# Shared PSUM bank for two transposes, head 0's weight sums on VectorE, and a later mLSTM turn

## Chip, cores and metric

The kernel runs on one core of a Trainium2 chip. The metric is the device time of one execution in microseconds (us), as the median of several runs.

## What is computed

One layer with two branches on the same RMS-normalised input (512 positions and 16 learned meta tokens, width 1024), merged by gates and projected:

```python
h = rms_norm(x, g_pre)
z = h @ w_in
(fq, fk, fv, ff, fz, mqk, mv, mi, mf, mo, mz, ga, gb) = jnp.split(z, SPLIT_POINTS, axis=-1)
...
ya = (oa * jax.nn.silu(fz)) @ w_a
...
hb = rms_norm(hb, g_head.reshape(MLSTM_HEADS, MLSTM_V_DIM)).reshape(B, L, MLSTM_WIDTH)
yb = (hb * jax.nn.silu(mz)) @ w_b
merged = jax.nn.sigmoid(ga) * ya + jax.nn.sigmoid(gb) * yb
return x + rms_norm(merged @ w_o, g_post)
```

`oa` is FoX attention: 8 heads of 128, softmax of scaled scores with a learned decay, in query chunks of 128. `hb` is the mLSTM: 4 heads with a matrix memory, in chunks of 128.

## The kernel before

Everything is float32, and each product is made of three matmuls of high and low parts (`mm3`, lines 149 to 152: high by high, high by low, low by high). Weights come by DMA on SP's queue into a ring of four raw buffers (`wload`, lines 122 to 129); ScalarE writes the high part, and VectorE subtracts it from the raw one for the low part (lines 142 and 144, and `split`, lines 250 and 252).

Many projections are Strassen units for 256 columns of the weights. `st_narrow` (from line 255) makes sums of blocks of the weights: two additions by the engine `adder` (lines 260 and 261) and two on VectorE (266 and 267); its splits are named `a`, `b`, `c` and `d`. `st_products` then runs seven products of 12 matmuls each, X, Y, Z, W, Y', X', Z', into two PSUM banks: X and Y use the second bank, Z and W the first. ScalarE takes snapshots of partial results: line 314 of the second bank after Y (Y' writes it again), 318 of the first after W, 322 of the second after X'. VectorE combines them at the end (325, 326, 328).

PSUM has eight banks, all of one pool and one tag (`psum1`); a new tile takes the bank that comes free first and waits until its last reader is done. A scheduler turns the program into one order for each engine, and an engine runs its instructions in that order. So both the order of the code and the bank that a tile happens to get set who waits for whom.

The first half of the program is the mLSTM, head by head. `mz_part` (lines 764 to 779) makes the gate `z` with two Strassen units for each head; `value_part` (781 to 813) makes the head's result (its matmuls are lines 790 to 792, from `w`, `wh` and `wl` of lines 728 to 731); `turn_part` (815 to 828) transposes the result on PE (821), multiplies it by the gate (824) and splits it (825, 826); and `wb_part` multiplies it by `w_b`. In head 0 ScalarE's line 742 evicts four banks `po`.

The second half is FoX attention, two heads at a time (`p` from 0 to 3, `m` 0 and 1). `fq_part`, `fk_part` and `fv_part` make queries, keys and values. `prob_part` reads the score banks `pl` on VectorE (line 972), takes the exponential on ScalarE (977) and writes probabilities `pn` on GpSimd and VectorE (980, 982). `ptr_part` (986 to 1006) transposes them on PE, chunk by chunk (996, and 997 for the meta tokens into `pmt`), and ScalarE and VectorE evict each chunk as high and low part (1001, 1002; 1003 and 1004 for `pmt`). `fout_part` multiplies them by the values (1016 to 1019, evicted by 1020). Between these stand Strassen units: `fz_part`, with a sigmoid on ScalarE (925) and a product on VectorE (926), and the gates `ga` and `gb` (`gate_part`, sigmoid in line 932). The seam between the halves is the code from `bt = turn_part(*pend)` on: the last head's transposes, the first `fq` unit, the first `fk`, `ga_part(0)`, `wb_part` of the last head and `gb_part(0)`.

```python
for c in range(NCH):
    o = OFFP[c]
    pt = psum1(f"pt{h}{c}")
    for j in range(c + 1):
        T.transpose(pt[:, j * P:(j + 1) * P], pn[:, o + P + j * P:o + P + (j + 1) * P], ident)
    T.transpose(pmt[:, c * P:(c + 1) * P], pn[:, o:o + P], ident)
```

Of the kernel before, what the change touches and what calls it, by code (L numbers as in the profile page):

```python
# [12 lines left out]
ALU = mybir.AluOpType  # L13

P = 128
# [11 lines left out]
MV = 512  # L27
# [5 lines left out]
C_MO, C_MZ, C_GA, C_GB = 8208, 10256, 12304, 13328  # L33
# [20 lines left out]
def tile_hybrid_block(ctx: ExitStack, tc: tile.TileContext, x, meta, norm_pre, norm_post, w_in, b_fox_f,  # L54
                      conv_w, conv_b, b_i, b_f, g_head, w_a, w_b, w_o, out):
    nc = tc.nc
    V, S, G, T = nc.vector, nc.scalar, nc.gpsimd, nc.tensor
# [8 lines left out]
    def f(ap):  # L66
        return ap.bitcast(F32)

    def psum1(name):
        return pa.tile([P, 512], F32, tag="pa", name=name)  # L70

    def banks(name, n):

        return [psum1(f"{name}_{i}") for i in range(n)]
# [6 lines left out]
    ident = cp.tile([P, 224], F32, name="ident")[:, 0:P]  # L81
# [16 lines left out]
    def sb(shape, dt, tag, name, pool=None, **kw):  # L98

        n = 1  # L100
        for d in shape[1:]:
            n *= d
        size = BYTES.get(tag, 4096)
        t = (pool or wk).tile([shape[0], size // (2 if dt == BF16 else 4)], dt, tag=tag, name=name, **kw)[:, 0:n]
        if len(shape) == 3:
            t = t.rearrange("p (a b) -> p a b", a=shape[1])
        elif len(shape) == 4:
            t = t.rearrange("p (a b c) -> p a b c", a=shape[1], b=shape[2])
        return t
# [23 lines left out]
    def wchunk(*args):  # L133

        return wsplit(wload(*args))
# [24 lines left out]
    def proj_t_all(ps, w, m, t0=0):  # L160

        n = (L - t0) // 2
        for u in range(2):
            s0 = t0 + u * n
            for k in range(KC):
                mm3(ps[u][:, 0:n], w[0](k, m * P, m * P + P), w[1](k, m * P, m * P + P),
                    hh[:, k, s0:s0 + n], hl[:, k, s0:s0 + n], k == 0, k == KC - 1)
# [121 lines left out]
    def st_products(o, units):  # L289


        begun = set()

        def prod(d, w, t):
            (wh_, wl_), (th, tl) = o[w], TB[t]
            for m, (wz, yx, _, ts) in enumerate(units):
                bank = wz if d in "WZ" else yx
                dst = bank[:, 0:256] if d in "WY" else bank[:, 256:512]
                first = (m, d in "WZ") not in begun
                begun.add((m, d in "WZ"))  # L300
                for k in range(4):
                    st, sp = first and k == 0, k == 3
                    if ts is None:
                        mm3(dst, wh_[:, k, :], wl_[:, k, :], th[:, k, :], tl[:, k, :], st, sp, skip_group_check=True)
                    else:
                        mm3(dst, th[:, k, ts], tl[:, k, ts], wh_[:, k, :], wl_[:, k, :], st, sp, skip_group_check=True)

        def halves(bank):
            return bank.rearrange("p (s n) -> p s n", s=2)

        prod("X", "a11", "b11")
        prod("Y", "s3", "t3")
        for wz, yx, snap, _ in units:
            S.activation(snap[:, 0:2], halves(yx), AF.Copy)
        prod("Z", "s1", "t1")
        prod("W", "a12", "b21")
        for wz, yx, snap, _ in units:
            S.activation(snap[:, 3], wz[:, 256:512], AF.Copy)
        prod("Y", "a22", "t4")
        prod("X", "s2", "t2")  # L320
        for wz, yx, snap, _ in units:
            S.activation(snap[:, 2], yx[:, 256:512], AF.Copy)
        prod("Z", "s4", "b22")
        for wz, yx, snap, _ in units:
            V.tensor_tensor(yx[:, 256:512], snap[:, 0], yx[:, 256:512], ALU.subtract)
            V.tensor_tensor(halves(yx), halves(yx), snap[:, 2:4], ALU.subtract)
        for wz, yx, snap, _ in units:
            V.tensor_tensor(halves(wz), halves(wz), snap[:, 1:3], ALU.add)
# [432 lines left out]
    def st_unit(c0, name, room, adder=V, into=None):  # L761

        ps = banks(f"p{name}", 2)
        st_products(st_narrow(c0, f"w{name}", adder, into), [(ps[0], ps[1], room.rearrange("p a (b n) -> p (a b) n", b=2), None)])
        return ps

    def mz_part(h, u):
        g = sb([P, 2, SEQ], F32, ("qk1h", "qk1l")[u], f"gz{h}{u}")
        into = None
        if u:  # L770
            t = sb([P, 2, 4, P], F32R, "sg", f"wz{h}{u}a", gp)
            into = t[:, 0], t[:, 1]
        ps = st_unit(C_MZ + h * MV + u * 256, f"z{h}{u}", g, G, into)
        for m in range(2):
            S.activation(g[:, m, :], ps[m], AF.Sigmoid)
        for m in range(2):
            mi = 80 + h * 4 + u * 2 + m
            V.scalar_tensor_tensor(g[:, m, :], ps[m], gc[:, mi:mi + 1], g[:, m, :], ALU.mult, ALU.mult)
        return g
# [34 lines left out]
    def turn_part(h, hts, gz):  # L814
        bh = sb([P, 4, SEQ], F32R, "big_h", f"bh{h}")
        bl = sb([P, 4, SEQ], F32R, "big_l", f"bl{h}")
        for c in range(NCH):
            pt = psum1(f"pht{h}{c}")
            pv = pt.rearrange("p (e t) -> p e t", e=4)
            for e_ in range(4):  # L820
                T.transpose(pv[:, e_, :], hts[c][:, e_ * P:(e_ + 1) * P], ident)
            y = sb([P, 4, P], F32, "y", f"yt{h}{c}", bufs=2)
            for u in range(2):
                V.tensor_tensor(y[:, 2 * u:2 * u + 2, :], pv[:, 2 * u:2 * u + 2, :], gz[u][:, :, c * P:(c + 1) * P], ALU.mult)
            S.activation(bh[:, :, c * P:(c + 1) * P], y, AF.Copy)
            V.tensor_tensor(bl[:, :, c * P:(c + 1) * P], y, f(bh[:, :, c * P:(c + 1) * P]), ALU.subtract)
        return bh, bl
# [19 lines left out]
    pend = None  # L847
    tokens = st_tokens()
    next(tokens)
    for h in range(MH):  # L850
        if pend is not None:
            bt = turn_part(*pend)
# [8 lines left out]
        if h == 0:  # L861
            v = v0
            ps = banks("pv01", 2)
# [19 lines left out]
        pend = (h, hts, gz)  # L883


    def fq_part(p):
        ps = st_unit(C_FQ + p * 256, f"fq{p}", sb([P, 2, SEQ], F32, "w", f"fqs{p}"))
        s = -(FD ** -0.5)
        qh = sb([P, 2, SEQ], F32R, "qk0h", f"fqh{p}")
        ql = sb([P, 2, SEQ], F32R, "qk0l", f"fql{p}")  # L890
        for m in range(2):
            S.activation(qh[:, m, :], ps[m], AF.Copy, scale=s)
            V.scalar_tensor_tensor(ql[:, m, :], ps[m], s, f(qh[:, m, :]), ALU.mult, ALU.subtract)
        return qh, ql

    def fk_part(p):
        w = wchunk(win, 0, KC, C_FK + p * 256, 256, f"wfk{p}")
        kh = sb([P, 2, L], F32R, "qk1h", f"fkh{p}")
        kl = sb([P, 2, L], F32R, "qk1l", f"fkl{p}")
        for m in range(2):  # L900
            ps = banks(f"pfk{p}{m}", 2)
            proj_t_all(ps, w, m)
            for u in range(2):
                hv = kh[:, m, u * HL:u * HL + HL]
                S.activation(hv, ps[u][:, 0:HL], AF.Copy)
                V.tensor_tensor(kl[:, m, u * HL:u * HL + HL], ps[u][:, 0:HL], f(hv), ALU.subtract)
        return kh, kl
# [77 lines left out]
    def ptr_part(p, m, pn):  # L985
        h = 2 * p + m
        pth = sb([P, NCH, SEQ], F32R, "big_h", f"pth{h}")
        ptl = sb([P, NCH, SEQ], F32R, "big_l", f"ptl{h}")
        ptm = sb([P, SEQ], F32R, "ptm", f"ptm{h}", gp)
        pmt = psum1(f"pmt{h}")  # L990
        pts = []
        for c in range(NCH):
            o = OFFP[c]
            pt = psum1(f"pt{h}{c}")
            for j in range(c + 1):
                T.transpose(pt[:, j * P:(j + 1) * P], pn[:, o + P + j * P:o + P + (j + 1) * P], ident)
            T.transpose(pmt[:, c * P:(c + 1) * P], pn[:, o:o + P], ident)
            pts.append(pt[:, 0:(c + 1) * P].rearrange("p (j t) -> p j t", t=P))
        for c, pv in enumerate(pts):
            dst = pth[:, 0:c + 1, c * P:(c + 1) * P]  # L1000
            S.activation(dst, pv, AF.Copy)
            V.tensor_tensor(ptl[:, 0:c + 1, c * P:(c + 1) * P], pv, f(dst), ALU.subtract)
        S.activation(ptm, pmt, AF.Copy)
        V.tensor_tensor(ptm[96:128, :], pmt[96:128, :], f(ptm[96:128, :]), ALU.subtract)
        return pth, ptl, ptm
# [24 lines left out]
        V.tensor_tensor(gl, yb[:, 2 * p:2 * p + 2, :], f(gh), ALU.subtract)  # L1030
        return gh, gl

    bt = turn_part(*pend)
    d_yb = [dram.tile([P, 2, SEQ], F32, name=f"d_yb{u}") for u in range(4)]
    d_sa = [dram.tile([P, 2, SEQ], F32, name=f"d_sa{u}") for u in range(3)]
    q = fq_part(0)
    k = fk_part(0)
    ga_part(0)
    wb_part(MH - 1, bt)
# [83 lines left out]
    pn = banks("pout", NCH)  # L1123
# [7 lines left out]
    for u in (2, 3):  # L1131
        w = wchunk(wo, 0, KC, u * 256, 256, f"wo{u}")
        for b in range(NCH):
            ps = psum1(f"pout{u}{b}")
# [40 lines left out]
```

## Time and profile before

| what | value |
|---|---|
| median of three runs | 946.1 us (945.33 to 946.22) |
| the profiled execution | 945.64 us, span 943.9 us |
| PE busy | 916.6 us, 97% of the span |
| VectorE (DVE) busy | 667.8 us, 71% |
| ScalarE (ACT) busy | 476.0 us, 50% |
| GpSimd (POOL) busy | 148.9 us, 16% |
| mean granted clock of PE | 0.992 of full speed |

The span runs from the first to the last instruction of the profiled execution; its own time has 1.7 us around it. In the rows further down, a line of a timeline gives the start, the length, the engine, the line of the program, the operation, the tiles (written <- read), the shape and, in brackets, how long the engine stood idle just before and whose result ended that. Several equal instructions in a row are one line with their number (x4). `PEclk` is the granted clock of PE as a share of full speed.

### The profile page before, as it was taken

To read this page: it belongs to the slowest core of one execution; us is meant where nothing else is said; L and a number is where in the kernel's file an instruction comes from. 1 tells how busy PE (TensorE), PEld (TensorE's weight loads), DVE (VectorE), ACT (ScalarE), POOL (GpSimd) and SP (SyncE) were. 2 spreads that over 40 slices of the span, in tenths; PEclk is the share of its full clock that TensorE was granted. 3 is DMA by queue.
4 is the path that set the end of the run, shared out by engine and by line. 5 is a ranking of instruction groups with operands and counts; after the bars stand their busy time and mean duration, and the time that the engine had idled before them with its cause. 6 is when DMAs were issued, how large, how long until landed. Compare 5 with 4: busy or idle time off the path is not lost.

```text
span 943.9 us, 15725 instructions
## 1 busy us (share of the span) xinstructions
PE 916.6 (97%) x6296; PEld 848.3 (90%) x6296; DVE 667.8 (71%) x1112; ACT 476.0 (50%) x818; POOL 148.9 (16%) x190
## 2 busy tenths in 40 slices
PE   8999799999999999999999999989999989999997
PEld 6998699889998899988999989889998989998887
DVE  6988678538887378874688757587885687895634
ACT  5746456435565255662465425455763554773331
POOL 3055100122001211012020002111321121300000
PEclk9999899999999999999999999999999999999999
DMA  7323132412333133233133335124362224348402
GB/s 229 92 71 108 45 112 73 121 42 76 104 113 93 53 90 90 91 101 90 26 109 90 113 111 158 52 75 135 90 193 75 75 67 135 97 169 317 139 23 90
DMA packets 73539, 97.47 MB, mean 103 GB/s; under 512 B 5237, under 2 KB 56533, under 8 KB 73466
## 3 DMA queue, kind: packets, MB, share of 16 engines
q1 hardware_dynamic: 71400, 92.76, 32.1%
q0 software_dynamic: 576, 2.10, 0.6%
q10 hardware_dynamic: 1490, 1.61, 0.5%
q8 instruction: 49, 0.80, 0.3%
q14 instruction: 24, 0.20, 0.1%
HBM read 90.62 MB, written 5.83 MB: 102 GB/s over the span
## 4 chain that ended last, share of the span: by engine, by line
PE 76%; DVE 11%; ACT 6%; issue 2%; POOL 2%; DMA 2%; POOLq 0%; DVEq 0%; ACTq 0%; SPq 0%
PE pyb L152 3%; PE pyb L150 3%; PE pyb L151 3%; PE pz L150 3%; PE pz L151 3%; PE pz L152 3%; PE pqk L150 3%; PE pqk L152 3%; PE pqk L151 3%; PE pv L152 3%; PE pv L150 3%; PE pv L151 3%; PE po L152 2%; PE po L151 2%; PE po L150 2%
## 5 line engine op out<-in xcount | busy, mean ns | idle before, releaser
L980 POOL TENSOR_SCALAR pn<-lt,rsum 128x128 f32<-128x128 f32 x32 | 28.4, 891 | 136.2 <-DVE rsum L978 99.5
L151 PE MATMUL pyb<-bl,wb_h 128*128 128x512 f32 x128 | 49.8, 389 | 0.0
L152 PE MATMUL pyb<-bh,wb_l 128*128 128x512 f32 x128 | 49.8, 389 | 0.0
L150 PE MATMUL pyb<-bh,wb_h 128*128 128x512 f32 x128 | 49.8, 389 | 0.0
L151 PE MATMUL pv<-wv_l,hh 128*128 128x512 f32 (+1 forms) x128 | 46.5, 364 | 1.5 <-DVE wv_l L144 1.5
L152 PE MATMUL pv<-wv_h,hl 128*128 128x512 f32 (+1 forms) x128 | 46.4, 363 | 0.0
L150 PE MATMUL pv<-wv_h,hh 128*128 128x512 f32 (+1 forms) x128 | 46.4, 362 | 0.0
L695 DVE SCALAR_TENSOR_TENSOR y<-z,gc,y 128x512 f32<-128x512 f32 (+1 forms) x48 | 36.2, 759 | 2.2 <-ACT y L688 1.5
L150 PE MATMUL pqk<-hh,wq_h 128*128 128x258 f32 x128 | 36.4, 284 | 0.0
L150 PE MATMUL pfk<-hh,wfk_h 128*128 128x264 f32 x128 | 36.3, 284 | 0.0
L150 PE MATMUL pqk<-hh,wk_h 128*128 128x264 f32 x128 | 36.3, 284 | 0.0
L151 PE MATMUL pfk<-hl,wfk_h 128*128 128x264 f32 x128 | 36.3, 284 | 0.0
L152 PE MATMUL pqk<-hh,wk_l 128*128 128x264 f32 x128 | 36.3, 283 | 0.0
L152 PE MATMUL pfk<-hh,wfk_l 128*128 128x264 f32 x128 | 36.3, 283 | 0.0
L151 PE MATMUL pqk<-hl,wk_h 128*128 128x264 f32 x128 | 36.2, 283 | 0.0
L152 PE MATMUL pqk<-hh,wq_l 128*128 128x258 f32 x128 | 36.0, 282 | 0.0
L151 PE MATMUL pqk<-hl,wq_h 128*128 128x258 f32 x128 | 36.0, 282 | 0.0
L151 PEld LDWEIGHTS pv<-wv_l,hh 128*128 128x128 f32 x128 | 24.1, 189 | 5.6 <-DVE wv_l L144 1.7
L845 DVE TENSOR_TENSOR yb<-pyb,yb 128x512 f32<-128x512 f32 x24 | 16.5, 688 | 17.4 <-PE pyb L152 17.4
L152 PEld LDWEIGHTS pyb<-bh,wb_l 128*128 128x128 f32 x128 | 24.0, 188 | 5.0
L151 PEld LDWEIGHTS pyb<-bl,wb_h 128*128 128x128 f32 x128 | 24.0, 188 | 4.9
L150 PEld LDWEIGHTS pyb<-bh,wb_h 128*128 128x128 f32 x128 | 24.0, 188 | 4.8
(1806 smaller groups left out, 3659.3 us busy)
## 6 DMA issues: line engine op xcount, KB each, us to landing
wv_r<-in_w_in_dram SPq DMA_DIRECT2D x16, 512.0 KB, 4.7
wo_r<-in_w_in_dram SPq DMA_DIRECT2D x16, 512.0 KB, 4.2
wz_r<-in_w_in_dram SPq DMA_DIRECT2D x16, 512.0 KB, 4.0
wb_r<-in_w_b_dram SPq DMA_DIRECT2D x16, 512.0 KB, 3.5
ab<-d_na SPq DMA_DIRECT2D x8, 672.0 KB, 4.0
wq_r<-in_w_in_dram SPq DMA_DIRECT2D x8, 512.0 KB, 3.7
wk_r<-in_w_in_dram SPq DMA_DIRECT2D x8, 512.0 KB, 4.2
wfq_r<-in_w_in_dram SPq DMA_DIRECT2D x8, 512.0 KB, 3.7
```

What stands on the lines that cost most here:

```text
L150: T.matmul(ps, ah, bh, start=start, stop=False, **kw)
L151: T.matmul(ps, ah, bl, start=False, stop=False, **kw)
L152: T.matmul(ps, al, bh, start=False, stop=stop, **kw)
L695: V.scalar_tensor_tensor(y[:, t0:L], z[:, m, t0 + j:L + j], gc[:, j * 16 + mi:j * 16 + mi + 1], y[:, t0:L], ALU.mult, ALU.add)
L845: V.tensor_tensor(dst, ps[i], dst, ALU.add)
L980: G.tensor_scalar(pn[:, o:o + P].rearrange("p (g t) -> p g t", g=4), lt[:, 0:32].unsqueeze(1).to_broadcast([P, 4, 32]), rsum, None, ALU.mult)
```

## The change

It has three parts. In `mz_part` the two units of head 0 make their additions of lines 260 and 261 on VectorE instead of GpSimd. In `ptr_part` the transposes of query chunks 0 and 1 go into one PSUM bank instead of two, with one filler transpose for the empty corner, and are evicted as one block of 2 x 256 instead of one of 128 and one of 256. And the last head's `turn_part` stands behind the first `fq` unit instead of ahead of it.

```diff
--- before.py
+++ after.py
@@ -770,7 +770,7 @@
         if u:
             t = sb([P, 2, 4, P], F32R, "sg", f"wz{h}{u}a", gp)
             into = t[:, 0], t[:, 1]
-        ps = st_unit(C_MZ + h * MV + u * 256, f"z{h}{u}", g, G, into)
+        ps = st_unit(C_MZ + h * MV + u * 256, f"z{h}{u}", g, G if h else V, into)
         for m in range(2):
             S.activation(g[:, m, :], ps[m], AF.Sigmoid)
         for m in range(2):
@@ -991,15 +991,21 @@
         pts = []
         for c in range(NCH):
             o = OFFP[c]
-            pt = psum1(f"pt{h}{c}")
+
+            if c != 1:
+                pt = psum1(f"pt{h}{c}").rearrange("p (j t) -> p j t", t=P)
             for j in range(c + 1):
-                T.transpose(pt[:, j * P:(j + 1) * P], pn[:, o + P + j * P:o + P + (j + 1) * P], ident)
+                T.transpose(pt[:, 1 + 2 * j if c == 1 else j, :], pn[:, o + P + j * P:o + P + (j + 1) * P], ident)
+                if c == 1 and j == 0:
+                    T.transpose(pt[:, 2, :], pn[:, o + P:o + P + P], ident)
             T.transpose(pmt[:, c * P:(c + 1) * P], pn[:, o:o + P], ident)
-            pts.append(pt[:, 0:(c + 1) * P].rearrange("p (j t) -> p j t", t=P))
-        for c, pv in enumerate(pts):
-            dst = pth[:, 0:c + 1, c * P:(c + 1) * P]
+            pts.append(pt)
+        pt2 = pts[1].rearrange("p (j c) t -> p j (c t)", j=2)
+        for pv, dst, low in ((pt2, pth[:, 0:2, 0:2 * P], ptl[:, 0:2, 0:2 * P]),
+                             *((pts[c][:, 0:c + 1], pth[:, 0:c + 1, c * P:(c + 1) * P],
+                                ptl[:, 0:c + 1, c * P:(c + 1) * P]) for c in (2, 3))):
             S.activation(dst, pv, AF.Copy)
-            V.tensor_tensor(ptl[:, 0:c + 1, c * P:(c + 1) * P], pv, f(dst), ALU.subtract)
+            V.tensor_tensor(low, pv, f(dst), ALU.subtract)
         S.activation(ptm, pmt, AF.Copy)
         V.tensor_tensor(ptm[96:128, :], pmt[96:128, :], f(ptm[96:128, :]), ALU.subtract)
         return pth, ptl, ptm
@@ -1030,10 +1036,10 @@
         V.tensor_tensor(gl, yb[:, 2 * p:2 * p + 2, :], f(gh), ALU.subtract)
         return gh, gl
 
-    bt = turn_part(*pend)
     d_yb = [dram.tile([P, 2, SEQ], F32, name=f"d_yb{u}") for u in range(4)]
     d_sa = [dram.tile([P, 2, SEQ], F32, name=f"d_sa{u}") for u in range(3)]
     q = fq_part(0)
+    bt = turn_part(*pend)
     k = fk_part(0)
     ga_part(0)
     wb_part(MH - 1, bt)
```

The lines of `ptr_part` and of what follows it move down: 996 becomes 998 (with 1000 for the filler), 997 becomes 1001, and the evictions of lines 1001 to 1004 become 1007 to 1010.

The first place is VectorE in head 0, where `wz00` and `wz01` belong to the two units (`wz_r` are the raw weights, `b_l` and `c_l` low parts).

```order
 L217 TENSOR_TENSOR t4l<-yb,t4h 128x1024
 L217 TENSOR_TENSOR t3l<-yb,t3h 128x1024
+L260 TENSOR_TENSOR wz_r_1253<-wz_r_1253 128x4x128
+L252 TENSOR_TENSOR wz01a<-wz_r_1428,wz01a 128x512
+L261 TENSOR_TENSOR wz_r_1253<-wz_r_1253,wz_r_1255 128x4x128
+L260 TENSOR_TENSOR wz_r_1428<-wz_r_1428 128x4x128
+L261 TENSOR_TENSOR wz_r_1428<-wz_r_1428,wz_r_1430 128x4x128
 L252 TENSOR_TENSOR wz00b_l<-wz_r_1253,wz00b_h 128x1024
 L252 TENSOR_TENSOR wz00c_l<-wz_r_1255,wz00c_h 128x1024
-L252 TENSOR_TENSOR wz01a<-wz_r_1428,wz01a 128x512
 L266 TENSOR_TENSOR wz_r_1255<-wz_r_1253,wz_r_1255 128x4x128
 L267 TENSOR_TENSOR wz_r_1255<-wz_r_1255 128x4x128
```

The four additions stand on VectorE behind line 217 and ahead of the low parts of the first unit, with `wz01a` among them.

The second place is ScalarE at the same time: `po` are the four banks that line 742 evicts, `wz00d_h` is the split of the sum that line 267 makes.

```order
 L250 ACTIVATE wz00b_h<-wz_r_1253 128x1024
 L250 ACTIVATE wz00c_h<-wz_r_1255 128x1024
-L250 ACTIVATE wz00d_h<-wz_r_1255 128x1024
 L742 ACT_TABLE_LOAD
 L742 ACTIVATE yb<-po_0_999 128x512
 L742 ACTIVATE yb<-po_1_1000 128x512
+L250 ACTIVATE wz00d_h<-wz_r_1255 128x1024
 L742 ACTIVATE yb<-po_2_1001 128x512
 L742 ACTIVATE yb<-po_3_1002 128x512
```

The table load and the first two evictions now stand ahead of `wz00d_h`.

The third place is PE at the second transposes of the first FoX pair (`p` 0, `m` 1), as it is after the change; before, each of the four chunks had a bank of its own (one, two, three and four transposes of line 996, each followed by one of line 997).

```order
L998 MATMUL pt_6550<-ident,pn_6354 128x128
L1001 MATMUL pmt_6549<-ident,pn_6354 128x128
L998 MATMUL pt_6550<-ident,pn_6354 128x128
L1000 MATMUL pt_6550<-ident,pn_6354 128x128
L998 MATMUL pt_6550<-ident,pn_6354 128x128
L1001 MATMUL pmt_6549<-ident,pn_6354 128x128
L998 MATMUL pt_6557<-ident,pn_6354 128x128 x3
L1001 MATMUL pmt_6549<-ident,pn_6354 128x128
L998 MATMUL pt_6562<-ident,pn_6354 128x128 x4
L1001 MATMUL pmt_6549<-ident,pn_6354 128x128
L150 MATMUL pgb_1_6578<-hh,wgb1a_h 128x256
```

Chunks 0 and 1 are in one tile, `pt_6550`, with the filler of line 1000 among them, and the `gb` unit's first product follows the last transpose as before.

## Rows read from the trace of the kernel before

**Rows 1.** PE's list of waits: what waited, releaser, total us, times, longest us.

```profile
PE pgb L150 <- DVE yb L926: 5.3, 2, 2.6
PE ps L150 <- ACT yb L742: 4.5, 1, 4.5
...
PE pfq L150 <- ACT sgb L932: 1.2, 1, 1.2
PE pfq L150 <- ACT fqs L314: 0.9, 1, 0.9
...
PE pga L150 <- ACT sga L318: 0.6, 1, 0.6
```

**Rows 2.** Windows: length, busy of PE, PEld, DVE, ACT, POOL; PEclk, DMA, GB/s.

```profile
109.00:113.00 4.00, 4.00 (x21) 4.00 (x22) 2.39 (x8) 0.63 (x1) 0.10 (x1) 0.57 0.00 0
624.50:628.50 4.00, 4.00 (x21) 4.00 (x22) 3.94 (x8) 2.06 (x5) 0.00 (x0) 0.57 0.35 119
88.00:98.00 10.00, 10.00 (x51) 8.57 (x50) 7.72 (x8) 3.23 (x4) 5.07 (x4) 1.00 0.01 2
600.00:845.00 245.00, 236.78 (x1800) 227.39 (x1799) 191.33 (x357) 142.28 (x253) 49.88 (x58) 0.99 0.33 103
```

**Rows 3.** Timeline of VectorE, head 0: start, us, instruction, idle before, releaser.

```profile
88.91 1.21 DVE L217 TENSOR_TENSOR t4l<-yb,t4h 128x1024 fp32r<-128x1024 f32 x1
90.04 2.31 DVE L217 TENSOR_TENSOR t3l<-yb,t3h 128x1024 fp32r<-128x1024 f32 x1
94.63 1.22 DVE L252 TENSOR_TENSOR wz00b_l<-wz_r,wz00b_h 128x1024 fp32r<-128x1024 f32 x1 [2.28 <-ACT wz00b_h L250]
...
98.23 1.64 DVE L267 TENSOR_TENSOR wz_r<-wz_r 128x512 f32<-128x512 f32 x1
...
106.53 0.69 DVE L731 TENSOR_TENSOR wl<-w,wh 128x512 fp32r<-128x512 f32 x1
```

**Rows 4.** Timeline of GpSimd, head 0.

```profile
89.07 2.20 POOL L260 TENSOR_TENSOR wz_r<-wz_r 128x512 f32<-128x512 f32 x1 [0.63 <-DVE wz00a_l L252]
```

**Rows 5.** Timeline of ScalarE, head 0.

```profile
99.98 1.06 ACT L250 ACTIVATE wz00d_h<-wz_r 128x1024 fp32r<-128x1024 f32 x1 [4.44 <-DVE wz_r L267]
101.06 1.28 ACT L742 ACT_TABLE_LOAD   x1
```

**Rows 6.** Timeline of VectorE, first `gb` unit of the FoX stretch.

```profile
613.67 0.69 DVE L260 TENSOR_TENSOR wgb_r<-wgb_r 128x512 f32<-128x512 f32 x1
...
623.66 1.29 DVE L926 TENSOR_TENSOR yb<-pfz,yb 128x512 f32<-128x512 f32 x2 [0.86 <-ACT yb L925]
```

**Rows 7.** Timeline of PE, head 0, line 790.

```profile
108.35 0.39 PE L790 MATMUL pnb<-vh,wh 128*128 128x258 f32 x1 [0.70 <-ACT wh L729]
```

**Rows 8.** Timeline of ScalarE at the seam.

```profile
543.05 0.63 ACT L250 ACTIVATE wgb0a_h<-wgb_r 128x512 fp32r<-128x512 f32 x1 [2.73 <-DMA wgb_r<-in_w_in_dram]
```

**Rows 9.** Timeline of PE, last transposes and first `gb` matmul.

```profile
621.15 0.60 PE L996 MATMUL pt<-ident,pn 128*128 128x128 f32 x4
621.58 0.27 PE L997 MATMUL pmt<-ident,pn 128*128 128x128 f32 x1
624.50 0.35 PE L150 MATMUL pgb<-hh,wgb1a_h 128*128 128x256 f32 x1 [2.64 <-DVE yb L926]
```

**Rows 10.** Timeline of ScalarE, the same unit and the `fq` unit.

```profile
624.00 1.44 ACT L1001 ACTIVATE pth<-pt 128x128 fp32r<-128x128 f32 x4
...
641.12 0.60 ACT L314 ACTIVATE fqs<-pfq 128x512 f32<-128x512 f32 x1 [0.16 <-POOL yb L939]
```

**Rows 11.** Timeline of VectorE, `fq` units of p = 1 and p = 2.

```profile
633.34 1.23 DVE L252 TENSOR_TENSOR wfq1c_l<-wfq_r,wfq1c_h 128x1024 fp32r<-128x1024 f32 x1 [0.95 <-ACT wfq1c_h L250]
...
696.37 1.23 DVE L252 TENSOR_TENSOR wfq2d_l<-wfq_r,wfq2d_h 128x1024 fp32r<-128x1024 f32 x1 [1.13 <-ACT wfq2d_h L250]
```

**Rows 12.** Timeline of PE, `fq` unit of p = 2.

```profile
697.66 0.28 PE L150 MATMUL pfq<-t2h,wfq2d_h 128*128 128x256 f32 x1
697.78 0.28 PE L151 MATMUL pfq<-t2l,wfq2d_h 128*128 128x256 f32 x1
```

## The prediction, on record before the run

> **What bounds the kernel now.** I read the list of waits first, then the three stretches that the change touches, each on TensorE (PE) and on the engine that PE waits for there. PE is busy for most of the span, so a saving shows in the time only where a wait of PE ends earlier. The long ones are few [rows 1]: 5.3 us before the gate units, in two waits, for VectorE's line 926; 4.5 us for ScalarE's line 742 in head 0; 1.2 us before a `fq` unit; 0.9 us at the seam for a snapshot of line 314. What such a wait costs is more than its own length: in the 4 us after the first of them, and after each of the two longest, the granted clock is near half instead of full, 0.57 of it in [rows 2]. By the clock that is 4.00 × 0.43 = 1.7 us; by the count, PE did 21 matmuls there where at its full step of about 0.118 us (0.12 between two rows, [rows 12]) it does 34, so 13 × 0.118 = 1.5. I take 1.6 us for one such slow stretch.
>
> **Part 1, head 0's weight sums on VectorE.** Before, the chain is this. GpSimd's first addition takes 2.20 us and starts beside VectorE's line 217, which then takes 2.31 us for what it did in 1.21 us one instruction earlier [rows 3, 4]. ScalarE's split of the sums, VectorE's, and the additions of lines 266 and 267 follow; line 267 takes 1.64 us beside GpSimd's second pair, ends at 99.87, and ScalarE, which waited 4.44 us for it, only then runs `wz00d_h`, loads a table (1.28 us) and gives PE its `po` bank back [rows 5]. PE goes on after 4.5 us [rows 1].
>
> After, GpSimd's four additions are gone and VectorE gets four: 4 × 0.69 = 2.76 us by line 260's duration in a FoX unit [rows 6]. It gets back (2.31 − 1.21) + (1.64 − 0.69) = 2.05 us of slowed work. Followed along the new order: line 217 ends at 91.2; the first pair with `wz01a` between, each 0.6 us apart, at 93.1; ScalarE's two splits at 95.15; and since the table load and the first two line 742 now stand ahead of `wz00d_h`, its first bank is free at 97.0, before PE asks for it at about 98.6. The 4.5 us wait goes. What is late next: the product of line 790 needs `wl` of line 731, which VectorE ends at 107.2 now. In the new order it does the second pair by 94.4, two splits by 96.7, lines 266 and 267 by 98.1, `wz00d_l` by 100.35, line 728 by 101.0, `wz01b_l` by 102.4, and starts line 731 there instead of at 106.53 [rows 3]: 4.1 us earlier. PE waits in three pieces for it and goes on 4.1 us earlier than 108.35 [rows 7]. The slow clock after that (0.57 in 109 to 113) I leave as it is, since PE still stands still before; the bounds are that it goes (+1.5) or grows (−1.5). **Term: +4.1, from 2.6 to 5.6.**
>
> A rule speaks against it. The Trainium skill (Perfetto Trace Analysis, Optimizing Scalar/DVE Operations) says that where VectorE is saturated some of its work may go to GpSimd, which would make this move the wrong way round. VectorE is busy 7.72 of 10 us in 88 to 98 [rows 2], and the rest is one wait of 2.28 us for ScalarE's split in this very chain [rows 3], so it is not saturated here; what the rule would give is rival 2.
>
> **Part 2, the seam: 0, from −2.0 to +0.9.** The transposes of `turn_part(3)` move behind the `fq` unit. Their 16 matmuls and all additions are the same; the unit starts earlier, its snapshot on ScalarE is no longer queued behind the two line 825, so the 0.9 us wait goes [rows 1]. But the `ga` unit after it waits for the snapshot of line 318, which stands on ScalarE behind `wgb0a_h`, and that waited 2.73 us for a weight transfer [rows 8]. The transfer's issue on SP's queue waits for a raw buffer that VectorE gives back, and VectorE has the same work in another order. So PE's lead is taken back there: the wait of 0.6 us grows to about 1.5. A slow clock after it would cost 1.6 more, and some tenths may be lost in VectorE's order: −2.0. If the transfer comes earlier too, +0.9 stays.
>
> **Part 3, the shared bank.** The place is the gate unit `gb` after a FoX pair's second transposes, at 621.69 and again at 758. All eight banks hold something there: two `pfz`, `pfo`, `pmt` and four `pt`. The unit's first bank is therefore `pfz`'s, and it waits for line 926 on VectorE, which waits for the sigmoid: 2.64 us, or 2.81 from 621.69, where the next matmul would have begun, to 624.50 [rows 9]. With one `pt` bank fewer the unit's first bank is that of a score tile that line 972 has read before line 260 starts at 613.67 [rows 6]. So PE starts its first two products at once, 24 matmuls × 0.118 = 2.8 us, until 624.5; the third needs `pfz`'s bank, which the first line 926 frees at about 624.35 [rows 6]. The whole 2.81 us and the slow stretch after it (1.6) go.
>
> Against it: one filler transpose in each of eight calls. Four of them (two for each place) lie on PE's busy path, 0.11 us each by four in 0.43 [rows 9]; at the others PE waits for line 972 or another engine anyway. The evictions cost the same: the four take 1.44 us on ScalarE [rows 10], and one of 512 columns takes the place of 128 and 256. The fourth product needs nothing new; the fifth writes the first bank, whose snapshot stands on ScalarE behind the evictions from 624.00, that of `pmt` and one split: with some 0.6 us for each of these and for itself it ends at 624.0 + 1.44 + 3 × 0.6 = 627.2, and PE asks for it at 627.4, just in time.
>
> What is late next is the following `fq` unit. PE reaches it about 4.1 us earlier, but VectorE only by its own waits for splits and snapshots that followed PE, 0.95 the longest [rows 11], some 1.5 in all. PE will want the snapshot of line 314, which ran at 641.12 [rows 10], at about 639.5, and gets it at about 640.2: a new wait of 0.6, with 0 and 1.2 as its ends. At the next boundary, p = 1 to 2, the 1.2 us wait for line 932 [rows 1] goes as well, but `wfq2d_l` ends at 697.60 and PE uses it at 697.66 [rows 11, 12]: VectorE sets the time there, and I count 0.
>
> So 2.81 + 1.6 − 0.22 − 0.6 = 3.6 at each of two places. **Term: +7.2, from 4.4 to 9.2.**
>
> The same page's section has a second rule against this: where ScalarE or VectorE isn't saturated but makes others wait, breaking instructions up may let work be done sooner, and here two are joined. At these two places the evictions start at 624.00, long after the transposes end at 621.85 [rows 9, 10]; by the rows joining costs nothing there.
>
> **Sum.** 4.1 + 0 + 7.2 = 11.3. The profiled execution took 945.64, so 934.3; the median of the three runs, 946.1, is 0.46 above it, so 934.8.
>
> **The rivals.**
> 1. *The freed bank does not help, or is given back at once.* For it: VectorE is busy 191 of 245 us in the FoX stretch [rows 2], and each lead of PE meets a chain through it. Against: both long waits end on line 926, and the 24 matmuls that can run meanwhile have their weights. Then only 4.1 − 4 × 0.11 = 3.7 is left: 942.4. Chance 0.12.
> 2. *VectorE is the bound in head 0*, and the four additions lengthen its chain by 2.76 − 2.05 = 0.7 instead of shortening it. Then 7.2 − 0.7 = 6.5: 939.6. Chance 0.06.
> 3. *The joined eviction is late.* It can start only when chunk 1's three transposes are there, 0.33 us later (3 × 0.11), and if PE then waits for what follows in all eight calls, 2.6 go: 937.4. Chance 0.04.
> 4. *Slower.* VectorE sets the pace of the whole FoX stretch: then the bank returns nothing, each of eight calls adds 0.11 on PE and 0.33 before the first eviction (3.5 in all), and head 0 loses 0.7. It decides where VectorE has no idle time of its own left; it has 54 us in 245 [rows 2], much of it while it waits for PE, which speaks against. 945.64 + 4.2 + 0.46 = 950.3. Chance 0.06.
> 5. *No change*: the scheduler's order gives all of it back at the seam and after. Chance 0.04.
>
> **How the numbers follow.** The forecast has 0.68. Its ends: the low one with the slow clock of head 0 gone (1.5), no new wait at the `fq` units (1.2) and the seam's 0.9 is 934.8 − 3.6 = 931.2; the high one with head 0's slow clock grown (1.5), the seam's 2.0 and one slow stretch kept in part 3 (1.6) is 939.9. 930.5 to 940.0 takes in rivals 2 and 3 and leaves out 1, 4 and 5, some 0.2. A measurement of this kernel can tell about 0.2%, 1.9 us. Faster by more than that: 0.68 + 0.12 + 0.06 + 0.04 = 0.90; same 0.04; slower 0.06.
>
> **What would show it.** Part 1: no wait for line 742 in head 0, and the second product of line 790 near 104.2; if it stands at 108 or later, rival 2. Part 2: the snapshot wait at 519 gone and the `ga` unit's for line 318 grown; no growth means +0.9. Part 3: no waits for line 926, a full clock in the stretches after, and a new short wait for line 314 in the `fq` units of p = 1 and 3; if the gate units start at once but PE loses as much within 20 us, rival 1. The prediction is wrong if the two gate units still wait over 1 us, or if PE's total of waits falls by less than 8 us.

## The result, and the profile after

The changed kernel takes 935.69 us (median of four executions, 934.46 to 938.23) against 945.89 us before (945.33 to 946.22): a ratio of 0.9896, 95% interval 0.9875 to 0.9918, so 10.2 us or 1.0% faster. The forecast was 934.8 us, its range 930.5 to 940.0.

The profile of the changed kernel was taken of its longest execution (938.23 us). That matters below. First the busy times:

```profile
PE 915.1 (98%) x6304; PEld 847.2 (90%) x6304; DVE 670.4 (72%) x1108; ACT 474.5 (51%) x810; POOL 141.6 (15%) x186
```

PE has eight transposes more than before, and yet is busy for less: 915.1 us against 916.6. The span is 7.5 us shorter. So 6.0 us of the gain are idle time of PE, and 1.5 us are work done at a higher granted clock (mean 0.995 instead of 0.992). Its waits (engine, line and tile waited for; total us, times, longest):

```profile
PE pnb L790 <- ACT wh L729: 2.8, 2, 2.1
PE pfq L150 <- ACT wfq2d_h L250: 1.9, 1, 1.9
...
PE pga L150 <- ACT sga L318: 1.3, 1, 1.3
PE pfq L150 <- ACT fqs L314: 1.2, 3, 0.5
PE pfq L152 <- DVE wfq2d_l L252: 0.8, 1, 0.8
PE pnb L792 <- DVE wl L731: 0.7, 1, 0.7
```

The 5.3 us for line 926 and the 4.5 us for line 742 of [rows 1] are gone, and so are the 1.2 us for line 932. In their place stand short waits (`fqs L314`, 0.5 us; `sga L318`, 1.3 instead of 0.6) and one of a size that was not forecast: 1.9 + 0.8 us for `wfq2d`. The three waits for `wh` and `wl`, 3.5 us together, are what is left of head 0's stop. Before, it was 6.0 us: the 4.5 us for line 742, and in the same list these two lines, which [rows 1] leaves out:

```profile
PE pnb L792 <- DVE wl L731: 0.8, 1, 0.8
PE pnb L790 <- ACT wh L729: 0.7, 1, 0.7
```

How PE's lead over the kernel before grows and shrinks can be read by comparing when the same matmul starts. The last column is a second profile of the very same kernel (experiment 1):

| PE starts | before | changed | lead | again | lead |
|---|---|---|---|---|---|
| head 0's scores (`ps`) | 94.69 | 94.86 | −0.17 | 94.91 | −0.22 |
| head 0's first `z` unit | 115.47 | 111.38 | 4.09 | 112.29 | 3.18 |
| `ga` unit after the seam, Z' | 544.00 | 539.61 | 4.39 | 540.49 | 3.51 |
| `fz` of p = 0, last product | 616.50 | 612.40 | 4.10 | 613.29 | 3.21 |
| `gb` after p = 0, third product | 628.93 | 620.50 | 8.43 | 621.40 | 7.53 |
| `fq` of p = 1, fifth product | 643.71 | 635.90 | 7.81 | 636.78 | 6.93 |
| `fq` of p = 2, first product | 690.62 | 681.71 | 8.91 | 682.89 | 7.73 |
| `fq` of p = 2, last product | 699.02 | 694.32 | 4.70 | 692.15 | 6.87 |
| `fz` of p = 2, last product | 753.56 | 749.42 | 4.14 | 746.97 | 6.59 |
| `gb` after p = 2, third product | 765.87 | 757.52 | 8.35 | 755.09 | 10.78 |
| `fq` of p = 3, fifth product | 780.57 | 772.91 | 7.66 | 770.48 | 10.09 |
| last `ga` unit, Z' | 847.68 | 840.26 | 7.42 | 837.94 | 9.74 |

Head 0, VectorE (what answers to [rows 3]):

```profile
89.36 1.21 DVE L217 TENSOR_TENSOR t4l<-yb,t4h 128x1024 fp32r<-128x1024 f32 x1
90.50 1.21 DVE L217 TENSOR_TENSOR t3l<-yb,t3h 128x1024 fp32r<-128x1024 f32 x1
91.63 0.68 DVE L260 TENSOR_TENSOR wz_r<-wz_r 128x512 f32<-128x512 f32 x1
...
97.88 0.69 DVE L267 TENSOR_TENSOR wz_r<-wz_r 128x512 f32<-128x512 f32 x1
...
102.82 0.68 DVE L731 TENSOR_TENSOR wl<-w,wh 128x512 fp32r<-128x512 f32 x1
```

Line 217 takes 1.21 us both times and line 267 0.69 instead of 1.64. Line 731 starts at 102.82, 3.7 us earlier than in [rows 3], or 3.9 when the 0.17 us by which this execution began later is taken off. ScalarE (as [rows 5]) loads the table and frees two `po` banks ahead of `wz00d_h`:

```profile
95.64 1.28 ACT L742 ACT_TABLE_LOAD   x1
96.93 1.09 ACT L742 ACTIVATE yb<-po 128x512 f32<-128x512 f32 x2
98.67 1.06 ACT L250 ACTIVATE wz00d_h<-wz_r 128x1024 fp32r<-128x1024 f32 x1 [0.65 <-DVE wz_r L267]
```

PE no longer waits for line 742 and stops at line 790 instead (as [rows 7]):

```profile
102.36 0.39 PE L790 MATMUL pnb<-vh,wh 128*128 128x258 f32 x1 [2.13 <-ACT wh L729]
...
104.64 0.58 PE L790 MATMUL pnb<-vh,wh 128*128 128x258 f32 x1 [0.70 <-ACT wh L729]
```

The FoX place (as [rows 9]): the `gb` unit starts with no wait behind the last transpose.

```profile
617.60 0.27 PE L1001 MATMUL pmt<-ident,pn 128*128 128x128 f32 x1
617.63 0.36 PE L150 MATMUL pgb<-hh,wgb1a_h 128*128 128x256 f32 x1
```

And the clock around it, and around the second such place, in the table of windows (length; busy PE, PEld, DVE, ACT, POOL; PEclk; DMA; GB/s). Full speed, 2.4 GHz, in both, where [rows 2] has 0.57 behind the first wait (0.59 behind the second, 761.5 to 765.5):

```profile
620.00:630.00 10.00, 10.00 (x83) 9.82 (x83) 8.71 (x14) 5.54 (x11) 0.00 (x0) 1.00 0.16 49
753.50:763.50 10.00, 10.00 (x89) 10.00 (x88) 8.55 (x13) 7.01 (x12) 0.61 (x2) 1.00 0.37 107
```

### The profile page after: what moved, and what is told of

It reads as the page before. It is cut to its first block, busy times and chain, and to the rows that moved or that the text cites. A ratio compares the mean times of both kernels' runs of the same rounds, so it can differ in the third digit from the quotient of the medians.

```text
span 936.4 us, 15730 instructions
## 1 busy us (share of the span) xinstructions
PE 915.1 (98%) x6304; PEld 847.2 (90%) x6304; DVE 670.4 (72%) x1108; ACT 474.5 (51%) x810; POOL 141.6 (15%) x186
## 4 chain that ended last, share of the span: by engine, by line
PE 81%; DVE 9%; ACT 5%; issue 2%; DMA 2%; POOL 1%; DVEq 0%; POOLq 0%; ACTq 0%; SPq 0%
PE pyb L151 3%; PE pyb L150 3%; PE pyb L152 3%; PE pz L150 3%; PE pz L151 3%; PE pz L152 3%; PE pqk L150 3%; PE pqk L152 3%; PE pqk L151 3%; PE pv L150 3%; PE pv L152 3%; PE pv L151 3%; PE po L152 2%; PE po L150 2%; PE po L151 2%
```

## Experiments

### 1. The changed kernel again

No edit. Expected:

> The changed kernel once more, for a second profile. The first one lost PE's lead at the query unit of the third pair (p = 2): VectorE's line 266 took 2.92 us there beside GpSimd's gate product (line 939), and PE waited 1.9 + 0.8 us for the split that follows. If that collision belongs to the order of the kernel, the second profile shows it again (line 266 over 2 us, PE's wait for wfq2d_h over 1.5 us) and its lead falls from about 8.9 to about 4.7 us there. If it is a matter of chance in one execution, line 266 takes about 0.7 us, the wait is under 1 us and the execution is some 2 to 4 us shorter, about 934 to 936.

Measured: 935.95 us (935.22 to 936.62, four executions), ratio 0.9892 (0.9872 to 0.9913) to the kernel before in the same comparison. The profiled execution took 935.91. The place in question in the first profile, VectorE:

```profile
683.58 2.92 DVE L266 TENSOR_TENSOR wfq_r<-wfq_r,wfq_r 128x512 f32<-128x512 f32 x1
686.42 1.74 DVE L1008 TENSOR_TENSOR ptl<-pt,pth 128x512 fp32r<-128x512 f32 x3
...
690.74 1.22 DVE L252 TENSOR_TENSOR wfq2d_l<-wfq_r,wfq2d_h 128x1024 fp32r<-128x1024 f32 x1 [1.12 <-ACT wfq2d_h L250]
```

GpSimd at that moment:

```profile
680.68 2.69 POOL L957 TENSOR_TENSOR ab<-ab,mask_q 128x128 f32<-128x128 f32 x4 [2.31 <-DMA ab<-d_na]
683.55 2.40 POOL L939 TENSOR_TENSOR yb<-yb,sgb 128x1024 f32<-128x1024 f32 x1 [0.17 <-ACT sgb L932]
```

And the same two in the second profile, VectorE:

```profile
684.49 0.77 DVE L266 TENSOR_TENSOR wfq_r<-wfq_r,wfq_r 128x512 f32<-128x512 f32 x1
685.18 1.74 DVE L1008 TENSOR_TENSOR ptl<-pt,pth 128x512 fp32r<-128x512 f32 x3
...
689.61 1.23 DVE L252 TENSOR_TENSOR wfq2d_l<-wfq_r,wfq2d_h 128x1024 fp32r<-128x1024 f32 x1 [1.13 <-ACT wfq2d_h L250]
```

GpSimd:

```profile
682.43 3.15 POOL L957 TENSOR_TENSOR ab<-ab,mask_q 128x128 f32<-128x128 f32 x4 [2.89 <-DMA ab<-d_na]
685.54 2.40 POOL L939 TENSOR_TENSOR yb<-yb,sgb 128x1024 f32<-128x1024 f32 x1
```

In the first execution GpSimd's gate product began at 683.55 and VectorE's line 266 at 683.58. Line 266 ended 0.55 us after the product did (683.55 + 2.40 = 685.95; 683.58 + 2.92 = 686.50): it stood still until GpSimd was through. In the second, GpSimd's line 957, which waits for a transfer, began later and took 0.5 us longer, so the product began only at 685.54, 1.05 us behind the start of line 266, when that was done. What ran on VectorE beside the product were evictions from PSUM, which take 1.74 us for three, the same as in the first profile, where they ran after the product. So the collision does not belong to the order of the kernel: which of the two starts first differs between executions. PE's lead fell from 8.91 to 4.70 in the one and from 7.73 to 6.87 in the other. That the unprofiled executions differ for the same reason is likely but not shown.

The Trainium skill (SBUF — State Buffer, Who interferes with whom) says that a VectorE instruction with two inputs in SBUF contends with a GpSimd instruction that reads SBUF, that this contention is an exclusive lock in which the order of issue decides who is blocked, and that VectorE's instructions with at most one input in SBUF, outside its two-port modes, do not contend. Both profiles agree, with the 2.92 and the 1.74 us.

### 2 to 4. Each part alone

Head 0's sums alone: the kernel before with

```diff
-        ps = st_unit(C_MZ + h * MV + u * 256, f"z{h}{u}", g, G, into)
+        ps = st_unit(C_MZ + h * MV + u * 256, f"z{h}{u}", g, G if h else V, into)
```

> Part 1 alone: head 0's four additions on VectorE, the rest as before. My theory (a chain through slow additions, not a saturated VectorE): the wait for line 742 goes and about 4.1 us remain at the end, 942 us. The rival that later stages take the lead back, since each of them has chains of its own: under 1 us faster than before.

Measured: 942.67 us, ratio 0.9963 (0.9948 to 0.9978), 3.6 us faster than 946.23 in the same comparison. PE's lead in its profile is −0.18 ahead of head 0's stop, 2.75 at the first `z` unit and still 2.51 at the last `ga` unit: the later stages take almost nothing of the 2.9 us back.

The shared bank alone: the kernel before with the change of `ptr_part` and nothing else.

> Part 3 alone: the shared bank, the rest as before. My theory: about 4 us at each of the two gate units, less 0.5 for the snapshot wait behind each, so 7 us if the query unit of p = 2 takes nothing back and 4 if it takes back the 3 that it took in the changed kernel's profile: 939 to 942 us. The rival that the bank gives nothing and the gain in the FoX stretch came from the other parts: 945 to 947 us.

Measured: 940.38 us, ratio 0.9943 (0.9923 to 0.9962), 5.9 us. In its profile the lead goes from −0.20 to 4.12 at the first `gb` unit and from 3.66 to 7.86 at the second, and is 6.87 at the last `ga` unit. PE's last matmul keeps that lead; the end of the program behind it took 1.1 us longer in this execution, so its span is 5.8 us shorter.

The seam alone: the kernel before with

```diff
-    bt = turn_part(*pend)
...
     q = fq_part(0)
+    bt = turn_part(*pend)
     k = fk_part(0)
```

> Part 2 alone: the last mLSTM transposes behind the first FoX unit. My theory: the 0.9 us wait goes and comes back at the gate unit ga, so 0 within 0.5 us: 946 us. The rival that it keeps what it gains: 945 us. The rival that a new wait slows PE's clock: 947 us or more.

Measured: 946.5 us, ratio 1.0001 (0.9991 to 1.0012). Its waits of PE:

```profile
PE pga L150 <- ACT sga L318: 1.2, 1, 1.2
...
PE pfq L150 <- ACT fqs L314: 0.2, 1, 0.2
```

Of the 0.9 us for `fqs L314` 0.2 are left, and the wait for `sga L318` is 1.2 instead of 0.6. At the `ga` unit the lead is 0.07. On ScalarE the split ahead of line 318 waits longer for the weight transfer, 3.34 us instead of 2.73 [rows 8]:

```profile
542.98 0.63 ACT L250 ACTIVATE wgb0a_h<-wgb_r 128x512 fp32r<-128x512 f32 x1 [3.34 <-DMA wgb_r<-in_w_in_dram]
```

So this part gives nothing and costs nothing, as forecast; the three parts alone sum to 3.6 + 5.9 − 0.3 = 9.2 us of the 10.2, equal within the intervals.

### 5. One more bank held

```diff
         pmt = psum1(f"pmt{h}")
+        held = psum1(f"held{h}")
...
                     T.transpose(pt[:, 2, :], pn[:, o + P:o + P + P], ident)
+                    T.transpose(held[:, 0:P], pn[:, o + P:o + P + P], ident)
...
+        S.activation(ptm[:, 0:4], held[:, 0:4], AF.Copy)
         S.activation(ptm, pmt, AF.Copy)
```

> The changed kernel, in which each of the eight transposition steps takes one more PSUM bank (written by one more transpose of 0.11 us, read by a ScalarE instruction of four columns only after the evictions), so that as many banks are live as before the change. Leaves nothing of the output out. My theory (the gain in the FoX stretch is the free bank and nothing else): the two waits for line 926 come back with 2.6 us each and the slow clock behind each, and the time is that of part 1 alone, 942.7, with up to 1 us more for the added instructions: 942 to 944 us. The rival that the gain came from the joined evictions or the new order: under 938 us.

Measured: 942.64 us, ratio 0.9972 (0.9958 to 0.9987). PE's waits for line 926 in its list:

```profile
PE pgb L150 <- DVE yb L926: 4.8, 2, 2.4
```

The joined evictions and the fillers are those of the changed kernel and the order is nearly its own; what is taken away is the bank. The two waits for line 926 are back, and between the last `fz` product of p = 0 and the `gb` unit behind it PE's lead over the kernel before does not change (2.27 and 2.27, where the changed kernel goes from 4.10 to 8.43). The free bank is the cause, and the time is that of head 0's part alone.

### 6. The gate product on VectorE

```diff
-        G.tensor_tensor(y, y, sg, ALU.mult)
+        (V if u == 2 else G).tensor_tensor(y, y, sg, ALU.mult)
```

> The changed kernel with the gate product of the third pair (line 939, u = 2 alone) on VectorE instead of GpSimd. It takes VectorE about 1.3 us there, and line 266 can no longer stand beside GpSimd's product (2.92 us in one profile, 0.77 in the other), nor line 267 (0.80, 1.29 before). My theory (VectorE's chain to the last split of the query unit sets the time there, by a hair): where there is no collision it is 1.3 us later than now and PE's wait grows from 0.6 to about 1.5 to 2, so 936.5 to 937.5; where there is one, it saves 1. On average 0 to +1.5 us against the changed kernel, and less spread. The rival that collisions cost in most executions: 1 to 2 us faster, 934 to 935.

Measured: 937.72 us (937.42 to 938.42, six executions), ratio 0.9923 (0.9906 to 0.9939): 2 us slower than the changed kernel, 0.2 us above the upper end of what was expected, and with the least spread of the kernels tried. In its profile PE waits 0.8 us for each of `wfq2d_h` and `wfq2d_l`, and its lead falls from 8.48 to 5.77 in this unit (7.73 to 6.87 in the second profile of the changed kernel). VectorE took 1.48 us for the product. So a sure 1.5 us on VectorE there is dearer than an occasional 2.2: that chain sets PE's time.

### 7. Not joined

Chunks 0 and 1 keep their shared bank, but are evicted one after the other, without a filler:

```diff
-                if c == 1 and j == 0:
-                    T.transpose(pt[:, 2, :], pn[:, o + P:o + P + P], ident)
...
-        pt2 = pts[1].rearrange("p (j c) t -> p j (c t)", j=2)
+        for c, pv in ((0, pts[0][:, 0:1]), (1, pts[1][:, 1:4:2]), (2, pts[2][:, 0:3]), (3, pts[3][:, 0:4])):
```

> The changed kernel with the shared bank kept but chunks 0 and 1 evicted one after the other, as before, and no filler transpose. My theory (the joined eviction starts long after the transposes at the places that matter): four fillers of 0.11 us less on PE, and about 0.2 us more on ScalarE and VectorE for each of eight calls, hidden but for the snapshot behind it, so 0 within 0.7 us: 935.2 to 936.6. The rival, that joining makes the others wait: 2.6 us faster, 933.3.

Measured: 936.57 us (935.1 to 937.04), ratio 0.9907 (0.989 to 0.9924). Not faster: joining the two evictions holds nothing up, and what the eight fillers cost is no more than what the added evictions do.

### 8 and 9. Half of head 0's sums

Only the first unit's additions on VectorE, then only the second's:

```diff
-        ps = st_unit(C_MZ + h * MV + u * 256, f"z{h}{u}", g, G if h else V, into)
+        ps = st_unit(C_MZ + h * MV + u * 256, f"z{h}{u}", g, G if h or u else V, into)
```

```diff
-        ps = st_unit(C_MZ + h * MV + u * 256, f"z{h}{u}", g, G if h else V, into)
+        ps = st_unit(C_MZ + h * MV + u * 256, f"z{h}{u}", g, V if h == 0 and u else G, into)
```

> The changed kernel with only the first z unit's two additions of head 0 on VectorE; the second unit's two are on GpSimd again. My theory (the gain of part 1 comes from the first unit: its additions and the ScalarE order that goes with them): PE's wait for line 742 stays away. VectorE is freed of two additions, 1.2 us, but GpSimd's pair runs beside VectorE's two-input instructions again and slows them by up to about 1 us each as line 217 and line 267 were slowed before: between 1.2 us faster and 1 us slower than the changed kernel, 934.5 to 937. The rival that the second pair on VectorE is what counts: the 4.5 us wait comes back, 939 to 940.

Measured: 937.77 us (935.96 to 939.05), ratio 0.9925 (0.991 to 0.994); the kernel before had 944.65 in this comparison.

> The reverse: only the second unit's additions on VectorE, the first unit's on GpSimd as before the change. My theory: GpSimd's first pair of 4.35 us still holds up the splits and slows line 217, the load of the table stays behind the last split, and PE's wait for line 742 is there again with 3 to 4.5 us: 938.5 to 940. The rival that line 267's slow execution beside the second pair was the cause: it takes 0.7 us instead of 1.64 and the wait falls to under 3 us, 936 to 938.

Measured: 940.18 us (938.63 to 940.6), ratio 0.9947 (0.9933 to 0.9961).

With the first unit's sums on VectorE the wait for line 742 stays away; but GpSimd's second pair runs beside VectorE's splits, and one of them takes 2.32 us instead of 1.22:

```profile
94.90 1.23 DVE L252 TENSOR_TENSOR wz00b_l<-wz_r,wz00b_h 128x1024 fp32r<-128x1024 f32 x1 [1.19 <-ACT wz00b_h L250]
96.04 2.32 DVE L252 TENSOR_TENSOR wz00c_l<-wz_r,wz00c_h 128x1024 fp32r<-128x1024 f32 x1
```

GpSimd in the same kernel:

```profile
94.94 2.33 POOL L261 TENSOR_TENSOR wz_r<-wz_r,wz_r 128x512 f32<-128x512 f32 x1
```

PE then waits 3.1 us for `wh` instead of 2.1. With the second unit's sums alone on VectorE, line 267 takes 0.68 us, as the rival said, but the wait is there again in PE's list:

```profile
PE ps L150 <- ACT yb L742: 4.2, 1, 4.2
```

The first is 0.8 us above its range, the second 0.2; against the kernel before, which was 1.2 us shorter in this comparison, it is 2.0 and 1.4. By the second line 790 PE has gained 2.9 us in the first and 0.3 in the second, where the seven profiles with all four additions on VectorE have 3.5 to 4.1. So the first unit's part gives most of the gain, and the second's next to nothing alone but about 1 us on top of the first, through the splits that GpSimd then no longer slows.

ScalarE in the first of the two kernels shows what the larger part hangs on:

```profile
95.83 1.28 ACT L742 ACT_TABLE_LOAD   x1
...
99.90 1.06 ACT L250 ACTIVATE wz00d_h<-wz_r 128x1024 fp32r<-128x1024 f32 x1 [1.69 <-DVE wz_r L267]
```

Here `wz00d_h` starts at 99.90, hardly sooner than in the kernel before (99.98, [rows 5]; 0.5 us sooner when the later start of this execution is taken off), and still the wait for line 742 is gone, because the table load stands ahead of it. In the second kernel the load stands behind it again, and the wait is back. So the wait goes by the order on ScalarE, which came with the first unit's additions. Whether that order alone would do as much, with all four additions left on GpSimd, no run shows. By the trace of the kernel before it could: ScalarE is through with `wz00c_h` at 94.50 + 1.04 = 95.54 there, and a load of 1.28 us and one eviction of about 0.6 would free the first bank near 97.4 (an estimate), before PE asks for it at 98.6.

### 10. Line 267 earlier at the third pair

An attempt to beat the changed kernel: `st_narrow` for `fq2` is written ahead of the transposes, so that line 267 comes behind the first eviction on VectorE and not behind all.

```diff
+        if p == 1:
+            early[2] = st_narrow(C_FQ + 2 * 256, "wfq2", V)
         pt1 = ptr_part(p, 1, pn1)
...
-            q = fq_part(p)
+            q = fq_part(p, early.pop(p, None))
```

> The changed kernel, in which the weight sums of the third pair's query unit (st_narrow for fq2) are written ahead of the transposes that precede it, so that VectorE runs line 267 behind the first eviction instead of behind all of them, about 2 us earlier; on ScalarE the snapshot of line 314 then stands behind two weight splits. My theory (what gives back PE's lead at this unit is line 267's place in VectorE's queue): the wait for wfq2d_l (0.6 to 0.8, and 1.9 more in the profile with a collision) goes, but PE then waits about 0.5 us for line 314, one product earlier: 0 to 1.5 us faster than the changed kernel, 934.3 to 936. The rival that another chain (keys' or values' weights) takes the lead back anyway: no difference, and the same lead at the end of the pair.

Measured: 936.95 us (934.22 to 938.13), ratio 0.9904 (0.9884 to 0.9923): no gain, and about 1 us above the range. In its profile the collision has only found another instruction, for line 267 now stands beside GpSimd's product. VectorE:

```profile
685.15 2.70 DVE L267 TENSOR_TENSOR wfq_r<-wfq_r 128x512 f32<-128x512 f32 x1
```

GpSimd:

```profile
684.91 2.39 POOL L939 TENSOR_TENSOR yb<-yb,sgb 128x1024 f32<-128x1024 f32 x1
```

The split that follows is as late as in the second profile (`wfq2d_h` starts 5.6 us behind the unit's first product in both), the snapshot of line 314 is queued behind it, and PE waits 2.3 us for that. The time without the collision was not seen in a profile, so whether the new order alone is worth something stays open. None of the other kernels beats the changed one.

## Why the prediction was right

**The sum.** Forecast 11.3 us, measured 10.2 by the medians. The second profile, whose execution is near the median, gives a lead of 9.74 at the end, and its steps stand to the forecast's so:

| step | forecast | second profile |
|---|---|---|
| later start of this execution | | −0.22 |
| part 1, head 0 | +4.1 | +3.40 |
| part 2, seam to the last `fz` product of p = 0 | 0 | +0.03 |
| part 3, first `gb` unit and the wait behind it | +3.6 | +3.72 |
| boundary p = 1 to 2 | 0 | −0.34 |
| part 3, second place | +3.6 | +3.50 |
| last pair | | −0.35 |

**One of its own signs of being wrong is met.** PE's total of waits was to fall by 8 us at least. The waits in its list add up to 20.3 us before, and to 14.5 and 13.1 in the two profiles of the changed kernel, so they fall by 5.8 and 7.2; by the idle time (span less busy time) it is 6.0 and 7.4. The forecast's sum comes to 8.5 us of waits (4.1 + 2 × 2.81 − 1.2) if part 1's whole 4.1 us are taken for waiting, and they are not: PE's waits in head 0 fall only by 2.5 us, from 6.0 to 3.5. Another 1.4 us by the second line 790 comes from the clock, since the six score matmuls that stood behind the wait for line 742 start about 0.43 us apart in the kernel before, at 1.2 GHz:

```profile
103.66 0.63 PE L151 MATMUL ps<-qkl,kr 128*128 128x512 f32 x1
104.08 0.63 PE L152 MATMUL ps<-qkh,kr 128*128 128x512 f32 x1
```

With no wait ahead of them they run at 2.4 GHz and start 0.23 us apart, here in the first profile:

```profile
98.91 0.39 PE L151 MATMUL ps<-qkl,kr 128*128 128x512 f32 x1
99.14 0.40 PE L152 MATMUL ps<-qkh,kr 128*128 128x512 f32 x1
```

The other sign is not met: the two gate units start without a wait. So the forecast's time holds, but its split into waiting and clock does not.

**Part 1** went by its steps: line 217 at full speed, the table load ahead, no wait for line 742, line 731 about 4 us earlier. The second line 790 starts at 104.64 in the first profile, 3.7 us before [rows 7] (forecast: 4.1, near 104.2). What was mis-sized is the slow clock. The forecast let it stand as it was with ±1.5; it differs between executions of the same program. These are the windows of three executions with the same head 0. The first profile of the changed kernel:

```profile
103.00:109.00 6.00, 4.75 (x25) 4.46 (x26) 4.34 (x12) 1.66 (x4) 0.10 (x1) 0.72 0.18 63
109.00:113.00 4.00, 4.00 (x36) 4.00 (x35) 2.91 (x10) 1.20 (x3) 0.56 (x1) 1.00 0.01 2
```

Its second profile:

```profile
103.00:109.00 6.00, 4.81 (x21) 4.42 (x21) 4.03 (x11) 1.66 (x4) 0.10 (x1) 0.50 0.21 73
109.00:113.00 4.00, 4.00 (x32) 4.00 (x32) 3.09 (x12) 0.72 (x2) 0.56 (x1) 0.91 0.01 2
```

Head 0's part alone:

```profile
103.00:109.00 6.00, 4.82 (x20) 4.34 (x20) 4.11 (x10) 1.66 (x4) 0.10 (x1) 0.56 0.21 74
109.00:113.00 4.00, 4.00 (x30) 4.00 (x29) 2.69 (x11) 0.72 (x2) 0.56 (x1) 0.80 0.01 2
```

Where the clock is at 2.4 GHz again by 109, PE leaves head 0 4.3 us earlier than before (4.09 + 0.17); where it stays longer at 1.2 GHz, 3.4 and 2.9. All seven profiles with this head 0 go the same way: 3.9 to 4.3 us with a granted clock of 1.00 in 109 to 113, 3.4 with 0.91, 2.7 to 2.9 with 0.77 to 0.80. So the term is 2.7 to 4.3, within its bounds but mostly under the value taken.

The forecast put the gain down to VectorE's chain. Experiments 8 and 9 show that the larger part comes with the order on ScalarE, which the forecast names as a step (the load ahead of `wz00d_h`) without giving it a price of its own. The Trainium skill's rule on offloading from a saturated VectorE (Perfetto Trace Analysis, Optimizing Scalar/DVE Operations) would have had the move the other way round, though the same passage adds that offloading between VectorE and GpSimd might not help. With the four additions VectorE is busy for 9.90 of 10 us in 88 to 98, and still the time falls.

**Part 2** is as forecast, shown by experiment 4: the gain at the snapshot goes into the `ga` unit's wait for line 318, and that into a longer wait for the weight transfer.

**Part 3** is as forecast, to a few tenths: 3.72 + 3.50 = 7.2 us in the second profile, and 7.2 forecast. Each `gb` unit gives 4.2 to 4.3 us (forecast 2.81 + 1.6 − 0.22 = 4.2), and the new wait for line 314 in the `fq` unit that follows is there with 0.54 and 0.52 us (forecast 0.6), PE in the first profile:

```profile
635.90 0.39 PE L150 MATMUL pfq<-t4h,wfq1c_h 128*128 128x256 f32 x1 [0.54 <-ACT fqs L314]
...
772.91 0.39 PE L150 MATMUL pfq<-t4h,wfq3c_h 128*128 128x256 f32 x1 [0.52 <-ACT fqs L314]
```

Experiment 5 shows that the bank is the reason. The second rule of the Trainium skill's section, that breaking instructions up may let work be done sooner, brought nothing here (experiment 7).

**The boundary p = 1 to 2** is where the working was too smooth. "VectorE sets the time there, and I count 0" holds for the second profile (1.4 us won at the wait for line 932, 1.7 lost ahead of it and behind it). But in the first the same place costs 4.8, from a lead of 8.91 to one of 4.14, because VectorE's line 266 starts 0.03 us behind GpSimd's product. The trace of the kernel before had the sign of it, on VectorE in the same unit, where line 267 took 1.29 us instead of 0.69:

```profile
693.95 1.29 DVE L267 TENSOR_TENSOR wfq_r<-wfq_r 128x512 f32<-128x512 f32 x1
```

What a moved chain will run beside belongs in the forecast.

**The rivals** fall: 1 by experiments 3 and 5 (the bank gives 5.9 us and they go with it), 2 by experiment 2, 3 by experiment 7, 4 and 5 by the time itself.

## What to carry to other kernels

When PE waits for an engine that only has to read a PSUM bank out, look which banks are live at that moment: one bank less in a helper nearby gave 4.2 us at each of two places, since the work that was ready could run and the clock stayed up. Additions that a helper engine does can be dearer there than on the busy engine: four of 0.68 us on VectorE took the place of GpSimd's of 1.6 to 2.2, beside which single VectorE instructions took about 1 us longer. But a moved instruction also changes the order on other engines, and in head 0 that gave more: read their order before naming the cause. And where a stage's lead is set by one engine with no slack, which of two instructions starts first decides over 2 us; take two profiles before explaining such a stretch.

## What was not expected of the hardware

VectorE's additions and subtractions with two SBUF inputs stood still for the rest of a GpSimd instruction that had begun before them (2.92 for 0.77 us, 2.70 for 0.69, 2.32 for 1.22), while evictions from PSUM beside the same GpSimd instruction kept their 1.74 us. And the length of the slow-clock stretch after the same short stops differs between executions of one program, by 1 us and more (the windows from 103 to 113 above). The Trainium skill (TensorE: Matmul & The Clock Gate, Part 1) says of a kernel's start that the number of slow matmuls varies from run to run; behind these stops in the middle of a kernel the rows show the same.
